# One product per rotation in the S5 scan, 64x64 matmul tiles for its states, and the attention scale moved to ScalarE

## The chip, the cores and the metric

The kernel runs on one core of a Trainium2 chip. The metric is device time in microseconds (us) of one execution, as the median of several; lower is better. Engine names are those of the profile: PE is the matmul engine, PEld its weight loads, DVE the vector engine, ACT the scalar engine, POOL the GpSimd engine, SP the engine that issues most DMAs.

## The reference, cut to what matters

The program computes two decoder layers on 512 tokens of width 1024. Each layer has a mixer (an S5 state-space group of 512 channels beside a differential-attention group of 4 heads) and a SwiGLU channel mixer. The two pieces that the change touches are the S5 recurrence and the last scale of an attention head:

```python
# S5: 32 groups of 16 channels, each with 64 complex states (separate real and imaginary arrays)
bu_re = einsum('blgc,gpc->blgp', u, bb_re); bu_im = einsum('blgc,gpc->blgp', u, bb_im)
# st[t] = lb * st[t-1] + bu[t], complex, for each group and state
y = einsum('blgp,gcp->blgc', st_re, c_re) - einsum('blgp,gcp->blgc', st_im, c_im) + d_skip * u
y = gelu(y);  y = y * sigmoid(y @ glu_w + glu_b)
...
# attention, per head and block of 128 queries
o = (softmax0 - lam * softmax1) @ v
o = o * rsqrt(mean(o * o) + RMS_EPS) * gain
```

## The kernel before

**Scan.** The 512 steps are cut into 64 blocks of 8. Inside a block everything is matmuls with tables (Q brings a block's inputs to the state, M is the block's own response, G brings the state that enters a block to the 8 outputs). Between blocks the state is multiplied by the 8th power of lb. `s5_scan` takes the phase of that factor out: it rotates the block inputs by a table of cosines and sines of k times the phase (k = 0 to 63), runs two real recurrences along k (`tensor_tensor_scan` with the magnitude `dt`), and rotates back. The 32 groups are treated in four quarters q of 8 groups; on the 128 partitions lie two groups of 64 states (g2 = 0, 1), and along the free axis four pairs of groups (a = 0 to 3) by 64 blocks.

A quarter runs in four steps, `inp`, `inT`, `scan` and `sout`. In `scan`, PE writes `vps` (real and imaginary part, 256 columns each) into PSUM. DVE makes four products of 256 columns and two sums for the first rotation, two scans, four products for the way back, and four sums of 64 partitions by 252 columns that write the states S, shifted by one block. S is 1024 columns wide: POOL has cleared it, and the states of g2 = 0 and g2 = 1 stand in different halves, so that `s5_out` can multiply all 128 rows of S by G at once (8 products of 128x128 by 128 columns; each float32 product is two instructions on PE).

**Tables.** `s5_rot` makes the cosines and sines of one quarter (POOL, DVE, ACT) and stores them in DRAM (`sC`, 512 columns). The store is issued from ACT's queue for layer 0 and from POOL's for layer 1. `s5_gen` loads them back into `csl` when a quarter begins. `s5_build` makes Q, G and the kernel of M. Layer 0's tables are built while its own attention starts; layer 1's during the channel mixer of layer 0.

**Buffers.** Tiles with one tag share a few buffers, and a new tile waits until the one whose buffer it takes is done with. `t5` has two buffers of 512 columns; it holds most short-lived tiles of the S5 part (`thl`, `cs`, `btmp`, `ta`, `ksb`, `stmp`, `gl`). `dt` has one of its own. `B` has four of 1024 columns (the inputs `u2`, the outputs `y`, and S), `XS` two of 1024 columns (`UU`, the transposed input, and `wz`, which holds rotated inputs and scanned states).

**Order.** While PE works through the q and k projections, a counter (`tick`) advances, and a table of due times (PLAN) says when the next step of `bld` (tables), `s5`, `att` (attention), `mod` (a column of the modulation: a 512 KB load and a DVE product) and `pf` (a weight unit: load, ACT copy `whi`, DVE difference `wlo`) is issued. An engine runs its instructions strictly in the order in which they are issued to it.

**Attention scale.** In `att_gen`, `scale(h)` computes one factor per query and block (`es`, its power of -1/2 on POOL), multiplies the four blocks of the head's output in PSUM by it on DVE (`on`), and `output(h)` transposes `on` on PE back into the same PSUM bank `po`.

Of the kernel before, what the change touches and what calls it, by code (L numbers as in the profile page):

```python
# [9 lines left out]
F32 = mybir.dt.float32  # L10
# [3 lines left out]
AF = mybir.ActivationFunctionType  # L14
# [48 lines left out]
def trunk_kernel(tc, xT, x, c, pos, modw, modb, wst, s5a, s5bc, s5d, glub, lamv, subw, lng, lnr, out):  # L63
# [3 lines left out]
    with ExitStack() as es:  # L67
# [9 lines left out]
        def u4(tag, shape, dt=F32, name=None):  # L77
            return up.tile(shape, dt, tag=tag, name=name or tag, bufs=BUFS[tag])
# [10 lines left out]
        def sm(shape, name, bufs=2):  # L89
            return sp.tile(shape, F32, tag=name, name=name, bufs=bufs)  # L90
# [80 lines left out]
                                pattern=[[-1, P]], channel_multiplier=1)  # L171
        maskb = cst.tile([P, P], BF16, name="maskb")
        nc.vector.tensor_copy(maskb, maskf)
        onesm = cst.tile([P, P], F32, name="onesm")
        nc.gpsimd.memset(onesm, 1.0)
        mask16 = cst.tile([P, 16], F32, name="mask16")
        nc.vector.tensor_reduce(mask16, ident.rearrange("p (b c) -> p c b", c=16), axis=AX.X, op=ALU.add)
        ebase = cst.tile([P, 16], F32, name="ebase")
# [70 lines left out]
        kd = [dp.tile([4, P, 240], F32, tag="kd", name=f"kd{l}") for l in range(L)]  # L249
        sG = dp.tile([4, P, 1024], F32, tag="sG", name="sG", bufs=1)  # L250
        sQ = dp.tile([4, P, 1024], F32, tag="sQ", name="sQ", bufs=1)
        sC = dp.tile([4, P, 512], F32, tag="sC", name="sC", bufs=1)
        xs = dp.tile([NT, P, D], F32, tag="xs", name="xs", bufs=1)

        def zero_pad(src):
# [244 lines left out]
        def s5_rot(l, q, pm):  # L500

            gs = slice(4 * q, 4 * q + 4)
            sh = [P, 4, 64]
            bg = lambda v: v[:, gs].rearrange("p (g o) -> p g o", o=1).to_broadcast(sh)
            kb = kio.rearrange("p (o k) -> p o k", o=1).to_broadcast(sh)
            thl = t5([P, 2] + sh[1:], name="thl")
            th, tl = thl[:, 0], thl[:, 1]
            tt(th, kb, bg(pm["hi"]), ALU.mult, eng=nc.gpsimd)
            tt(tl, kb, bg(pm["lo"]), ALU.mult, eng=nc.gpsimd)
            cs = t5([P, 2, 4, 64], name="cs")  # L510
            ct, st = cs[:, 0], cs[:, 1]
            flat = lambda v: v.rearrange("p g k -> p (g k)")
            ts(ct, th, INV2PI, ALU.mult, MAGIC, ALU.add)
            ts(ct, ct, MAGIC, ALU.subtract)
            for v, c_ in ((th, -T1), (tl, -T2)):
                stt(flat(v), flat(ct), c_, flat(v), ALU.mult, ALU.add)
            tt(th, th, tl, ALU.add)
            ts(th, th, PI_LO, ALU.min, -PI_LO, ALU.max)
            sincos(ct, st, th, nc.vector)
            getattr(nc, "gpsimd" if l else OPT["CSQ"]).dma_start(sC[q], cs.rearrange("p r g k -> p (r g k)"))  # L520

        tabs = {}

# [44 lines left out]
        def s5_scan(l, q, U, Q, cs):  # L568

            gs = slice(4 * q, 4 * q + 4)  # L570
            ct, st = cs[:, 0], cs[:, 1]
            dt = sm([P, 4, 64], "dt", 1)
            nc.gpsimd.tensor_copy(dt, pms[l]["r8"][:, gs].rearrange("p (g o) -> p g o", o=1).to_broadcast([P, 4, 64]))
            nc.gpsimd.memset(dt[:, :, 0:1], 0.0)
            vps = ps5("vps")
            for ri in range(2):
                for a in range(4):
                    for g2 in range(2):
                        nc.tensor.matmul(vps[64 * g2 : 64 * g2 + 64, ri * 256 + 64 * a : ri * 256 + 64 * a + 64],
                                         Q[:, a, ri, 64 * g2 : 64 * g2 + 64],  # L580
                                         U[:, a, 64 * g2 : 64 * g2 + 64],
                                         start=True, stop=True, tile_position=(0, 64 * g2))
            v = vps.rearrange("p (r a k) -> p r a k", r=2, a=4)
            wz = u4("XS", [P, 4, 4, 64], name="wz")
            tmp = t5([P, 2, 4, 64], name="stmp")
            tt(tmp[:, 0], v[:, 0], ct, ALU.mult)
            tt(tmp[:, 1], v[:, 1], st, ALU.mult)
            tt(wz[:, 0], tmp[:, 0], tmp[:, 1], ALU.add)
            tmp = t5([P, 2, 4, 64], name="stmp")
            tt(tmp[:, 0], v[:, 1], ct, ALU.mult)  # L590
            tt(tmp[:, 1], v[:, 0], st, ALU.mult)
            tt(wz[:, 1], tmp[:, 0], tmp[:, 1], ALU.subtract)
            flat = lambda v_: v_.rearrange("p g k -> p (g k)")
            for ri in range(2):
                nc.vector.tensor_tensor_scan(flat(wz[:, 2 + ri]), flat(dt), flat(wz[:, ri]), 0.0,
                                             op0=ALU.mult, op1=ALU.add)
            S = u4("B", [P, 2, 4, P], name="S")
            nc.gpsimd.memset(S, 0.0)
            for ri in range(2):
                tmp = t5([P, 2, 4, 64], name="stmp")  # L600
                tt(tmp[:, 0], wz[:, 2 + ri], ct, ALU.mult)
                tt(tmp[:, 1], wz[:, 3 - ri], st, ALU.mult)
                for g2 in range(2):
                    rows = slice(64 * g2, 64 * g2 + 64)
                    tt(S[rows, ri, :, 64 * g2 + 1 : 64 * g2 + 64], tmp[rows, 0, :, 0:63], tmp[rows, 1, :, 0:63],
                       ALU.subtract if ri == 0 else ALU.add)
            return S

        def s5_out(q, U, S, G, M, y):
            hh = q % 2  # L610
            ps = ps5("yps")

            for a in range(4):
                for g2 in range(2):
                    nc.tensor.matmul(ps[64 * g2 : 64 * g2 + 64, a * P : (a + 1) * P],
                                     U[:, a, 64 * g2 : 64 * g2 + 64], M[:, 2 * a + g2],
                                     start=a == 0, stop=False, tile_position=(0, 64 * g2))
            for a in range(4):
                for ri in range(2):
                    mm(ps[:, a * P : (a + 1) * P], S[:, ri, a], G[:, a, ri], False, a == 3 and ri == 1)  # L620
            yo = y.rearrange("p i (g c) -> p g i c", g=8)[:, 4 * hh : 4 * hh + 4]

            gl = t5([P, 512], name="gl")
            nc.scalar.activation(gl, ps, AF.Square, scale=GELU_C)
            stt(gl, gl, 1.0, ps, ALU.add, ALU.mult)
            nc.scalar.activation(gl, gl, AF.Tanh, scale=GELU_S)
            stt(gl, gl, 1.0, ps, ALU.add, ALU.mult)
            cp(yo, gl.rearrange("p (a i c) -> p a i c", a=4, i=8), scale=0.5)
# [11 lines left out]
        def s5_gen(l, u2, us, yh, yl):  # L640
            src = u2[0][:, 0:1]
            U, S, Q, C, GM, y = {}, {}, {}, {}, {}, {}

            def inp(q):
                if l:
                    Q[q] = s5_load_q(l, q, us[0][:, 0:1] if q == 0 else src)
                U[q] = s5_in(u2, q)
                C[q] = sm([P, 2, 4, 64], "csl", 1)
                nc.sync.dma_start(C[q].rearrange("p r g k -> p (r g k)"), sC[q])

            def inT(q):
                U[q] = s5_inT(U[q])

            def scan(q):
                if l == 0:
                    Q[q] = tabs[q]["Q"]
                GM[q] = s5_load_gm(l, q, src)
                S[q] = s5_scan(l, q, U[q], Q[q], C[q])

            def sout(q):  # L660
                if q % 2 == 0:
                    y[q // 2] = u4("B", [P, 8, P], name="y")
                s5_out(q, U[q], S[q], *GM[q], y[q // 2])

            def yT(b, ih):
                if (b, ih) == (0, 0):
                    for i in range(2):
                        yh[i] = u4("A1", [P, 2, T], F32R, name="yh")
                        yl[i] = u4("A1", [P, 2, T], F32R, name="yl")
                s5_yT(y[b], b, ih, yh, yl)  # L670

            seq = [(fn, (q,)) for q in range(4) for fn in (inp, inT, scan, sout)]
            seq += [(yT, (b, ih)) for b in range(2) for ih in range(2)]
            for fn, args in seq:
                fn(*args)
                yield
# [42 lines left out]
        def att_gen(qkts, vt, nlam, gain, mix):  # L719
# [57 lines left out]
            def scale(h):  # L777

                g = hd[h]
                ss, q2, po = g["ss"], g["q2"], g["po"]  # L780
                es_ = sm([P, NT], "es", 2)
                tt(es_, ss[:, :, 0], ss[:, :, 0], ALU.mult)
                ts(es_, es_, EPS * P, ALU.mult)
                tt(es_, es_, q2, ALU.add)
                ts(es_, es_, 1.0 / P, ALU.mult)
                tt(es_, es_, mhalf.to_broadcast([P, NT]), ALU.pow, eng=nc.gpsimd)
                on = ta_([P, NT, P], name="on")
                for i in range(NT):
                    ts(on[:, i], po[:, i * P : (i + 1) * P], es_[:, i : i + 1], ALU.mult)
                g["on"] = on  # L790

            def output(h):
# [569 lines left out]
```

## Time and profile before

| | |
|---|---|
| median of 3 runs | 1278.39 us (1275.9 to 1282.51) |
| profiled execution, its own time | 1279.54 us |
| its span in the trace | 1277.8 us |
| busy: PE, DVE, ACT, POOL | 1190.9, 841.6, 478.9, 206.4 us |
| mean granted PE clock | 0.976 of full speed |

The span is what the trace shows from the first instruction to the last; 1.74 us of the execution's own time lie around it. Busy shares are means over stages with different limits, so a stage is read by its own window. In a timeline row stand the start, the time from the first instruction's start to the last one's end, the engine and line, and in brackets the engine's idle time before it with what ended it.

### The profile page before, as it was taken

What the parts mean: (1) busy time and instruction counts of PE and PEld (TensorE: products, weight loads), DVE (VectorE), ACT (ScalarE), POOL (GpSimd) and SP (SyncE); (2) the same over time, 40 slices, a digit from 0 to 9 for tenths busy, and PEclk for the clock granted to TensorE, in tenths of its full rate; (3) what the DMA queues carried; (4) which work ended last, traced back from release to release, by engine and by line L of the source; (5) the groups of instructions that cost most, each with busy time, mean ns of one, the idle gap of its engine ahead of it and who ended that gap; (6) DMA issues with size and microseconds to landing.
All of it is one profiled execution on the core that took longest, in us unless ns stands there. A gap on an engine that the chain in (4) does not pass through costs nothing.

```text
span 1277.8 us, 17430 instructions
## 1 busy us (share of the span) xinstructions
PE 1190.9 (93%) x6608; PEld 992.1 (78%) x6608; DVE 841.6 (66%) x1537; ACT 478.9 (37%) x846; POOL 206.4 (16%) x286
## 2 busy tenths in 40 slices
PE   4768888999999999989899999999999999999997
PEld 3557777688888888867687798878888888888885
DVE  6679999866687576698647557785666222235556
ACT  3413446527322222243346245661733222234330
POOL 8943320001002121132001131100000000000001
PEclk8887999999999999999899999999999999999999
DMA  9654236534665666744333554423463333333241
GB/s 357 226 153 143 65 82 226 158 107 152 195 221 186 226 200 193 252 141 146 117 99 101 186 168 107 131 83 99 151 196 103 98 96 100 99 99 115 66 133 66
DMA packets 66868, 186.57 MB, mean 146 GB/s; under 512 B 7936, under 2 KB 21536, under 8 KB 66784
## 3 DMA queue, kind: packets, MB, share of 16 engines
q1 hardware_dynamic: 62352, 174.88, 43.4%
q0 software_dynamic: 2848, 8.70, 2.1%
q10 hardware_dynamic: 1584, 1.88, 0.5%
q8 instruction: 52, 0.85, 0.3%
q14 instruction: 32, 0.26, 0.1%
HBM read 171.85 MB, written 11.49 MB: 143 GB/s over the span
## 4 chain that ended last, share of the span: by engine, by line
PE 68%; DVE 18%; DMA 4%; POOL 3%; issue 3%; ACT 3%; SPq 0%; DVEq 0%; POOLq 0%; ACTq 0%
PE gps L116 37%; PE dps L116 14%; PE ops L116 4%; PE vps L116 3%; DVE mraw L110 3%; PE ups L116 2%; PE qkps L116 2%; DVE wlo L104 2%; DVE stmp L104 1%; POOL s5tmp L104 1%; DMA mraw<-in_modw 1%; DMA wraw<-in_wst 1%; DVE Gt L104 1%; PE yps L116 1%; PE glups L116 1%
## 5 line engine op out<-in xcount | busy, mean ns | idle before, releaser
L104 DVE TENSOR_TENSOR wlo<-wraw,whi 128x1024 fp32r<-128x1024 f32 x180 | 225.3, 1254 | 266.3 <-ACT whi L113 264.4
L113 ACT ACTIVATE whi<-wraw 128x1024 fp32r<-128x1024 f32 x184 | 194.2, 1058 | 376.6 <-PE gps L116 273.0
L116 PE MATMUL gps<-hT2h,whi 128*128 128x512 f32 (+1 forms) x768 | 286.4, 373 | 0.2
L116 PE MATMUL gps<-hT2l,whi 128*128 128x512 f32 (+1 forms) x768 | 285.7, 372 | 0.0
L116 PE MATMUL gps<-hT2h,wlo 128*128 128x512 f32 (+1 forms) x768 | 285.3, 372 | 0.0
L116 PE MATMUL dps<-whi,ah 128*128 128x512 f32 x704 | 223.7, 397 | 8.2 <-DVE rtmp L104 4.5
L116 PEld LDWEIGHTS gps<-hT2h,whi 128*128 128x128 f32 x768 | 144.6, 188 | 25.8 <-DVE rtmp L104 0.6
L116 PEld LDWEIGHTS dps<-whi,ah 128*128 128x128 f32 x704 | 133.9, 190 | 39.5 <-DVE rtmp L104 6.0
L116 PEld LDWEIGHTS gps<-hT2h,wlo 128*128 128x128 f32 x768 | 144.7, 188 | 25.1
L116 PEld LDWEIGHTS gps<-hT2l,whi 128*128 128x128 f32 x768 | 144.7, 188 | 24.9
L116 PE MATMUL dps<-wlo,ah 128*128 128x512 f32 x352 | 138.5, 393 | 0.0
L110 DVE SCALAR_TENSOR_TENSOR mraw<-mraw,scb 128x1024 f32<-128x1024 f32 x96 | 122.0, 1299 | 1.8 <-DMA mraw<-in_modw 1.6
L113 ACT ACTIVATE ah<-aT 128x512 fp32r<-128x512 f32 x88 | 53.8, 627 | 115.5 <-PE dps L116 93.2
L104 DVE TENSOR_TENSOR ah<-aT,ah 128x512 fp32r<-128x512 f32 x88 | 61.1, 706 | 40.0 <-ACT ah L113 39.6
L116 PEld LDWEIGHTS dps<-wlo,ah 128*128 128x128 f32 x352 | 67.2, 191 | 13.6
L116 PE MATMUL qkps<-whi,hTh 128*128 128x256 f32 x128 | 39.7, 312 | 7.3 <-ACT whi L113 6.5
L116 PE MATMUL ops<-whi,am 128*128 128x512 f32 x128 | 43.4, 398 | 0.0
L116 PE MATMUL qkps<-wlo,hTh 128*128 128x256 f32 x128 | 40.0, 313 | 0.5 <-DVE wlo L104 0.5
L104 POOL TENSOR_TENSOR rs<-rs,mhalf 128x1 f32<-128x1 f32 x16 | 10.8, 676 | 176.8 <-DVE rs L101 176.8
L116 PE MATMUL qkps<-whi,hTl 128*128 128x256 f32 x128 | 39.1, 306 | 0.0
L751 ACT ACTIVATE e<-sps,nm 128x128 f32<-128x128 f32 (+3 forms) x64 | 33.1, 525 | 14.9 <-DVE nm L749 12.8
L116 PE MATMUL qkps<-whi,hTnh 128*128 128x256 f32 x128 | 37.4, 292 | 0.0
(290 smaller groups left out, 1939.4 us busy)
## 6 DMA issues: line engine op xcount, KB each, us to landing
wraw<-in_wst SPq DMA_DIRECT2D x184, 512.0 KB, 3.7
mraw<-in_modw SPq DMA_DIRECT2D x96, 512.0 KB, 4.8
M<-kd SPq DMA_DIRECT2D x64, 64.0 KB, 3.6
gb<-in_lnr SPq DMA_DIRECT2D x8, 512.0 KB, 4.1
xT<-in_xT SPq DMA_DIRECT2D x8, 256.0 KB, 7.1
u<-us SPq DMA_DIRECT2D x32, 64.0 KB, 2.5
csl<-sC SPq DMA_DIRECT2D x8, 256.0 KB, 2.8
x<-in_x SPq DMA_DIRECT2D x4, 512.0 KB, 4.1
```

The lines of the kernel that those rows point to most:

```text
L104: (eng or nc.vector).tensor_tensor(out, a, b, op=op)
L110: nc.vector.scalar_tensor_tensor(out, a, s, b, op0=ALU.mult, op1=ALU.mult, accum_out=acc_out)
L113: nc.scalar.activation(out, in_, AF.Copy, scale=scale)
L116: nc.tensor.matmul(ps, a, b, start=start, stop=stop)
L751: nc.scalar.activation(e[:, m, :n], ps[:, m, :n], AF.Exp, bias=nm[:, m : m + 1], accum_out=ss[:, i, m : m + 1])
```

## The change

- The table of a quarter gets a third part: minus sine, cosine, sine, side by side (768 columns). `s5_rot` makes the minus sine with one more DVE operation into a new `t5` tile and stores it with a second DMA.
- A rotation is one DVE product of 1024 columns: the input (512 columns) is read twice, and the table is read as two overlapping windows of 512 columns. The product `rp` takes a buffer of tag `B`. The first rotation then needs one sum of 512 columns; the second needs two sums of 252 columns over all 128 partitions. The real and imaginary parts are kept in the other order between the two rotations.
- The states S are plain (64 columns per group pair, no zero halves) and overwrite the first half of `wz`. POOL clears only the first column of each block instead of 1024 columns.
- `s5_out` multiplies S by G in tiles of 64 rows by 64 columns of the array, one for each g2: 16 products instead of 8.
- `dt` becomes a `t5` tile; the scan's `stmp` tiles are gone.
- `scale(h)` multiplies the four blocks on ACT instead of DVE.
- An unused constant tile of ones is no longer made.

```diff
-        onesm = cst.tile([P, P], F32, name="onesm")
-        nc.gpsimd.memset(onesm, 1.0)
...
-        sC = dp.tile([4, P, 512], F32, tag="sC", name="sC", bufs=1)
+        sC = dp.tile([4, P, 768], F32, tag="sC", name="sC", bufs=1)
...
-            getattr(nc, "gpsimd" if l else OPT["CSQ"]).dma_start(sC[q], cs.rearrange("p r g k -> p (r g k)"))
+            ns = t5([P, 256], name="ns")
+            ts(ns, flat(st), -1.0, ALU.mult)
+            eng = getattr(nc, "gpsimd" if l else OPT["CSQ"])
+            eng.dma_start(sC[q][:, 256:768], cs.rearrange("p r g k -> p (r g k)"))
+            eng.dma_start(sC[q][:, 0:256], ns)
...
-            dt = sm([P, 4, 64], "dt", 1)
+            dt = t5([P, 4, 64], name="dt")
...
-            wz = u4("XS", [P, 4, 4, 64], name="wz")
-            tmp = t5([P, 2, 4, 64], name="stmp")
-            tt(tmp[:, 0], v[:, 0], ct, ALU.mult)
-            tt(tmp[:, 1], v[:, 1], st, ALU.mult)
-            tt(wz[:, 0], tmp[:, 0], tmp[:, 1], ALU.add)
...
-            S = u4("B", [P, 2, 4, P], name="S")
-            nc.gpsimd.memset(S, 0.0)
-            for ri in range(2):
-                tmp = t5([P, 2, 4, 64], name="stmp")
-                tt(tmp[:, 0], wz[:, 2 + ri], ct, ALU.mult)
-                tt(tmp[:, 1], wz[:, 3 - ri], st, ALU.mult)
-                for g2 in range(2):
-                    rows = slice(64 * g2, 64 * g2 + 64)
-                    tt(S[rows, ri, :, 64 * g2 + 1 : 64 * g2 + 64], tmp[rows, 0, :, 0:63], tmp[rows, 1, :, 0:63],
-                       ALU.subtract if ri == 0 else ALU.add)
+            two = [P, 2, 2, 256]
+
+            def rot_of(v):
+                rows_ = bass.AP(cs.tensor, cs.offset, [cs.ap[0], [256, 2], [256, 2], [1, 256]])
+                pr = u4("B", two, name="rp")
+                tt(pr, v.rearrange("p (o j x) -> p o j x", o=1, j=2).to_broadcast(two), rows_, ALU.mult)
+                return pr
+
+            wz = u4("XS", [P, 4, 256], name="wz")
+            pr = rot_of(vps)
+            tt(wz[:, 0:2], pr[:, :, 0], pr[:, :, 1], ALU.add)
+            d1 = dt.rearrange("p g k -> p (g k)")
+            for o in range(2):
+                nc.vector.tensor_tensor_scan(wz[:, 2 + o], d1, wz[:, o], 0.0, op0=ALU.mult, op1=ALU.add)
+            pr = rot_of(wz[:, 2:4].rearrange("p j x -> p (j x)"))
+            S = wz[:, 0:2].rearrange("p o (g k) -> p o g k", g=4)
+            nc.gpsimd.memset(S[:, :, :, 0:1], 0.0)
+            for o in range(2):
+                po, pj = (pr[:, o, j].rearrange("p (g k) -> p g k", g=4)[:, :, 0:63] for j in range(2))
+                tt(S[:, o, :, 1:64], po, pj, ALU.add)
...
-                    mm(ps[:, a * P : (a + 1) * P], S[:, ri, a], G[:, a, ri], False, a == 3 and ri == 1)
+                    for g2 in range(2):
+                        rows_ = slice(64 * g2, 64 * g2 + 64)
+                        nc.tensor.matmul(ps[rows_, a * P : (a + 1) * P], S[rows_, ri, a], G[rows_, a, ri],
+                                         start=False, stop=a == 3 and ri == 1, tile_position=(64 * g2, 64 * g2))
...
-                C[q] = sm([P, 2, 4, 64], "csl", 1)
-                nc.sync.dma_start(C[q].rearrange("p r g k -> p (r g k)"), sC[q])
+                C[q] = sm([P, 768], "csl", 1)
+                nc.sync.dma_start(C[q], sC[q])
...
-                    ts(on[:, i], po[:, i * P : (i + 1) * P], es_[:, i : i + 1], ALU.mult)
+                    nc.scalar.activation(on[:, i], po[:, i * P : (i + 1) * P], AF.Copy, scale=es_[:, i : i + 1])
```

## Rows read from the trace of the kernel before

**Rows 1.** The page, busy time of each engine and its share.

```profile
PE 1190.9 (93%) x6608; PEld 992.1 (78%) x6608; DVE 841.6 (66%) x1537; ACT 478.9 (37%) x846; POOL 206.4 (16%) x286
```

**Rows 2.** Busy time by stage; first row names columns.

```profile
core 0: us, PE busy (x) PEld busy (x) DVE busy (x) ACT busy (x) POOL busy (x), PEclk, DMA share, GB/s
64.00:110.00 46.00, 34.54 (x234) 30.24 (x232) 35.35 (x77) 10.44 (x20) 18.08 (x23) 0.81 0.50 143
110.00:235.00 125.00, 106.74 (x937) 91.36 (x936) 118.04 (x254) 60.73 (x146) 28.05 (x27) 0.95 0.43 127
235.00:265.00 30.00, 27.82 (x153) 21.11 (x152) 22.03 (x54) 14.14 (x40) 3.49 (x3) 1.00 0.56 173
534.00:612.00 78.00, 70.49 (x364) 56.15 (x362) 68.60 (x109) 29.69 (x46) 23.61 (x25) 0.98 0.47 149
740.00:852.00 112.00, 106.30 (x929) 94.11 (x928) 80.38 (x194) 61.44 (x155) 20.53 (x24) 1.00 0.42 119
```

**Rows 3.** Timeline of DVE: first and last operations of two scans, layer 0.

```profile
110.53 1.08 DVE L104 TENSOR_TENSOR stmp<-vps,csl 128x256 f32<-128x256 f32 x3
...
115.03 1.82 DVE L104 TENSOR_TENSOR S<-stmp 64x252 f32<-64x252 f32 x4
...
141.19 0.76 DVE L104 TENSOR_TENSOR stmp<-vps,csl 128x256 f32<-128x256 f32 x2 [1.42 <-PE vps L579]
...
146.43 2.52 DVE L104 TENSOR_TENSOR S<-stmp 64x252 f32<-64x252 f32 x4
```

**Rows 4.** Groups by form: busy us, mean ns of one, idle before.

```profile
L104 DVE TENSOR_TENSOR wlo<-wraw,whi 128x1024 fp32r<-128x1024 f32 x180 | 225.3, 1254 | 266.3 <-ACT whi L113 264.4 <-DMA M<-kd 1.5
...
L104 DVE TENSOR_TENSOR gluy<-yh,yl 128x512 f32<-128x512 f32 x8 | 5.5, 688 | 0.0
...
L104 DVE TENSOR_TENSOR wz<-stmp 128x256 f32<-128x256 f32 x16 | 6.6, 410 | 0.0
...
L101 DVE TENSOR_SCALAR on<-po,es 128x128 f32<-128x128 f32 x32 | 9.5, 345 | 6.9 <-POOL es L104 6.9
...
L751 ACT ACTIVATE e<-sps,nm 128x128 f32<-128x128 f32 x16 | 5.7, 366 | 5.0 <-DVE nm L749 5.0
...
L598 POOL MEMSET S<- 128x1024 f32 x8 | 7.6, 953 | 0.0
```

**Rows 5.** Instructions of tile wz: duration ns min/median/max.

```profile
L595 DVE TENSOR_TENSOR_SCAN wz<-dt,wz x16: 680/684/2883, 112.2 to 808.1; 128x256 f32<-128x256 f32 x16
```

**Rows 6.** Timeline of PE around a quarter's output, layer 1.

```profile
815.13 1.09 PE L615 MATMUL yps<-M,UU 128*64 128x128 f32 x16
816.15 2.05 PE L116 MATMUL yps<-G,S 128*128 128x128 f32 x16
...
819.38 0.94 PE L747 MATMUL sps<-qk 64*128 64x128 f32 x12
```

**Rows 7.** Timeline of ACT: next quarter's input, then this quarter's output.

```profile
115.15 0.63 ACT L113 ACTIVATE UU<-u 128x512 f32<-128x512 f32 x1 [7.48 <-DVE stmp L104]
...
121.41 0.60 ACT L624 ACTIVATE gl<-yps 128x512 f32<-128x512 f32 x1 [3.56 <-PE yps L116]
```

**Rows 8.** Instructions of tile cs: duration ns min/median/max; landing of its DMA.

```profile
L101 DVE TENSOR_SCALAR cs<-cs x16: 281/294/708, 67.1 to 603.8; 128x256 f32<-128x256 f32 x16
...
L520 POOL DMA_DIRECT2D sC<-cs x4: 562/572/583, 451.9 to 604.6; - x4
...
DMA to landing us min/median/max: 2.0/2.6/4.4
```

**Rows 9.** Timeline of ACT, DVE and POOL where tables are built, layer 0.

```profile
78.09 0.33 ACTq L520 DMA_DIRECT2D sC<-cs  x1
...
78.03 0.22 DVE L104 TENSOR_TENSOR btmp<-s5bc,kre 128x64 f32<-128x64 f32 x1
...
104.54 1.11 POOL L104 TENSOR_TENSOR ta<-pw,s5bc 128x512 f32<-128x512 f32 x1 [4.94 <-DMA sC<-cs]
```

More of the change, by code (lines that the diff above doesn't have):

```diff
@@ L570, in s5_scan @@
             gs = slice(4 * q, 4 * q + 4)
-            ct, st = cs[:, 0], cs[:, 1]
-            dt = sm([P, 4, 64], "dt", 1)
+            dt = t5([P, 4, 64], name="dt")
             nc.gpsimd.tensor_copy(dt, pms[l]["r8"][:, gs].rearrange("p (g o) -> p g o", o=1).to_broadcast([P, 4, 64]))
@@ L582, in s5_scan @@
                                          start=True, stop=True, tile_position=(0, 64 * g2))
-            v = vps.rearrange("p (r a k) -> p r a k", r=2, a=4)
-            wz = u4("XS", [P, 4, 4, 64], name="wz")
-            tmp = t5([P, 2, 4, 64], name="stmp")
-            tt(tmp[:, 0], v[:, 0], ct, ALU.mult)
-            tt(tmp[:, 1], v[:, 1], st, ALU.mult)
-            tt(wz[:, 0], tmp[:, 0], tmp[:, 1], ALU.add)
-            tmp = t5([P, 2, 4, 64], name="stmp")
-            tt(tmp[:, 0], v[:, 1], ct, ALU.mult)
@@ L591, in s5_scan @@
-            tt(tmp[:, 1], v[:, 0], st, ALU.mult)
-            tt(wz[:, 1], tmp[:, 0], tmp[:, 1], ALU.subtract)
-            flat = lambda v_: v_.rearrange("p g k -> p (g k)")
-            for ri in range(2):
-                nc.vector.tensor_tensor_scan(flat(wz[:, 2 + ri]), flat(dt), flat(wz[:, ri]), 0.0,
-                                             op0=ALU.mult, op1=ALU.add)
-            S = u4("B", [P, 2, 4, P], name="S")
-            nc.gpsimd.memset(S, 0.0)
-            for ri in range(2):
-                tmp = t5([P, 2, 4, 64], name="stmp")
-                tt(tmp[:, 0], wz[:, 2 + ri], ct, ALU.mult)
-                tt(tmp[:, 1], wz[:, 3 - ri], st, ALU.mult)
-                for g2 in range(2):
-                    rows = slice(64 * g2, 64 * g2 + 64)
-                    tt(S[rows, ri, :, 64 * g2 + 1 : 64 * g2 + 64], tmp[rows, 0, :, 0:63], tmp[rows, 1, :, 0:63],
-                       ALU.subtract if ri == 0 else ALU.add)
+            two = [P, 2, 2, 256]
```

## The prediction

> **What bounds the kernel now.** I read the page first: PE is busy 93% of the span and DVE 66% [rows 1], which says only that most of the program is PE's. Then the windows by stage, because the edits touch four stages [rows 2]. In 110 to 235 us, layer 0's attention and scans, DVE is busy 118.04 of 125 us (94%) and PE 106.74 at a clock of 0.95: DVE sets the pace there. In 534 to 612 us, where layer 1's last tables are built, DVE is busy 68.60 of 78 (88%) and PE idles 7.5 us. In 740 to 852 us, layer 1's attention and scans, PE is busy 106.30 of 112 and DVE 80.38: PE sets the pace, and no relief of another engine can give more than the 5.7 us in which PE idles. Between 64 and 110 us neither is full (DVE 35.35 of 46, PE 34.54); this stage is a chain of table building. So an edit is worth nearly its DVE time in layer 0's attention, at most a few us in layer 1's, and its waits count in the table building.
>
> **The scan on DVE.** Before, two scans of layer 0 took 115.03 + 1.82 - 110.53 = 6.3 us and 146.43 + 2.52 - 141.19 = 7.8 us of DVE, from first product to last sum [rows 3]; the second includes an operation of the attention. After, seven operations remain, each (but the second scan and the last sum) needing the one before: a product of 1024 columns (1.25 us, from the 1024-column difference), a sum of 512 (0.69), two scans (0.68 each), a product of 1024 (1.25), two sums of 252 (0.41 each, from a 256-column sum) [rows 4, 5]. Together 5.4 us. No row has a DVE operand that is read twice or by overlapping windows, nor 1024 columns of PSUM by SBUF. If that costs nothing, the saving is 6.3 - 5.4 = 0.9 to 7.8 - 5.4 = 2.4 us a quarter; if the product from PSUM took twice its price, 1.25 more, it would be -0.3 to 1.1. I take 1.5: what an operation does is still one element per lane and step, and the four half-partition sums, which stretch to 2.52 us in the second scan, become two. That is 6 us of DVE in each layer. POOL's clearing of S (0.95 us each) goes too [rows 4]; POOL is idle most of that stage, so I count nothing for it.
>
> **The attention scale.** Four DVE operations of 0.345 us, 1.4 us a head, go to ACT, where a 128x128 operation from PSUM with a per-partition operand takes 0.366 us [rows 4]: four take 1.5 us. ACT is busy 60.73 of 125 us in layer 0 and 61.44 of 112 in layer 1 [rows 2], so it has room; but it runs in order, and a 1 us copy ahead of it can delay `on`, then PE's transposes. The chain's length stays the same within 0.1 us, and DVE is relieved of 1.4 us a head: 3 heads inside layer 0's full stage, 4.1 us; 4 heads in layer 1.
>
> **What that relief is worth.** Layer 0: 6 + 4.1 = 10.1 us of DVE. All of it counts if DVE alone sets the pace; but PE has only 18 us of room in 110 to 235, and the last stretch, 235 to 265, has DVE at 22.03 of 30 [rows 2]. I take three quarters: -7.6 us (bounds -10.1 and, by one third, -3.4). Layer 1: 11.5 us of DVE, but PE has 5.7 us to give: I take -2.5 (bounds -5.7 and 0).
>
> **The longer table.** One more DVE operation for each quarter and layer, 0.29 us as the 256-column scalings of `cs` [rows 8], and one more DMA issue: 0.33 us on ACT's queue in layer 0 [rows 9], 0.57 us on POOL in layer 1 [rows 8]. Layer 0 does it in the table building, where ACT's next weight copy is queued behind the issue: 4 x (0.29 + 0.33) = 2.5 us, of which I put 0.5 on the path, since neither engine is full. In layer 1, 4 x 0.29 = 1.2 us of DVE, mostly in or near a stretch that is DVE's own: +1.0. The load of `csl` grows from 256 to 384 KB; it is issued a step ahead of the scan, and I price it at nothing while that step covers it; uncovered, it would cost half of a like transfer's time again, about 1.3 us (half of 2.6) [rows 8].
>
> **The new wait.** The table's third part is a `t5` tile, and `t5` has two buffers. The sequence was thl, cs, next tile: the next tile took thl's buffer, free as soon as ACT had read it. Now it is thl, cs, ns, next tile: ns takes thl's buffer, and the next tile must wait for the store of cs to land. In layer 0 the first products of the table build stand right there: DVE starts `btmp` at 78.03, while ACT issues the store of cs at 78.09 [rows 9]; it lands 2.6 us later (median) [rows 8]. So `btmp` would start at about 78.09 + 2.6 = 80.7, 2.7 us late, and behind it in DVE's queue stand the products of G, on which PE's next tables wait. The third and fourth quarter's tables come right before the next build in the same way; there POOL's `ta` already waits 4.94 us for such a landing [rows 9], so part is paid already: +1.3. Sum +4.0; bounds 0 (other DVE work is issued into the gap: DVE has 10.6 us of idle time in 64 to 110) and +8 (each of three tables costs 2.7). In layer 1, steps of the build lie several us apart and POOL's queue holds the stores; I count the landing as covered. `dt`, now in `t5` too, takes over one of the two buffers until the second scan is done; the `stmp` tiles held both, so I count nothing.
>
> A second wait moves: S now lives in `wz`, so the next quarter's `UU` on ACT can no longer take that buffer when the last product has read it (it did, at 115.15, after 7.48 us of ACT waiting) but only after PE's output product, which ended just before 121.41 [rows 7]. Behind it on ACT are weight copies. This quarter's own `gl` waits for the same PE product, so an order that places `UU` beside `gl` loses nothing; I take 0 (bounds 0 and 6 us once, if the copies stay behind `UU`).
>
> **PE's products.** The old 16 instructions with S took about (2.05 - 0.28)/15 = 0.12 us each, a last 0.28 taken off as the duration of a single one [rows 6]. The new 32 work on two different quarters of the array. Pairs of column tiles, writing the two halves of the same PSUM bank, go at (1.09 - 0.28)/15 = 0.054 us each, and pairs of row tiles, in two different banks, at (0.94 - 0.28)/11 = 0.06 [rows 6]. At that rate 32 take 1.7 to 1.9 us beside 1.8: no change. If the pairs did not overlap, 32 x 0.12 = 3.8 us: +2.0 us a quarter. I take 0, since the two tiles write different partitions.
>
> Here the Trainium skill speaks against the change: TensorEngine Tiling (Array Packing), section Restrictions and Gotchas, says that different row tiles cannot access the same PSUM bank at the same time. The new products are row tiles of one bank; by that rule they would take turns, and the sum would be the one of rival D below. No row of before has such a pair.
>
> **Sum.** -7.6 - 2.5 + 0.5 + 1.0 + 4.0 + 0 = -4.6 us. The profiled execution took 1279.54 us, so its like would take 1274.9; the runs' median is 1.15 us lower, 1278.39, which gives 1273.8. I say 1274.
>
> **Rivals.** About 0.5%, 6.4 us, is what a measurement of this kernel can tell from no change: faster is below 1272.0, slower above 1284.8.
>
> A, the sum above, 1270 to 1279: 0.44.
>
> B, the relief counts whole and the new wait is filled: -10.1 in layer 0, -4 in layer 1, +2.0 for the table: -12, 1266. For it: DVE at 94% for 125 us; against it: a PE near its limit too. 0.22.
>
> C, slower by the two `t5` buffers: the waits for the stores cost 8 + 1.5, and since tables come later, PE idles, falls to the lower of its two clock levels (1.2 instead of 2.4 GHz), and only a third of layer 0's relief (-3.4) arrives, none in layer 1: +6, 1284.5, split evenly around the bound. It decides from the point where the store's landing costs more than DVE saves in layer 0, some 7.6 us. For it: the clock of 0.81 in 64 to 110 and a PE that already lacks work there [rows 2]; against it: DVE's idle time there. 0.22.
>
> D, the 64x64 pairs take turns: +2.0 x 4 = 8 in layer 1, where PE sets the pace, and a quarter of that, 2, in layer 0: -4.6 + 10 = +5.4, 1283.8. For it: no row of a like pair; against it: the pairs of column tiles that share a bank. 0.12.
>
> Faster: B and 0.14 of A, 0.36. Slower: half of C and a little over half of D, 0.11 + 0.07 = 0.18. Same: what is left, 0.46. The range that leaves out no more than 2 in 10 goes from 1264 (B and a little) to 1287 (C and D with their spread).
>
> **What would show it.** Scans of 5.4 us on DVE; `on` on ACT at 0.37 us; the 32 S products in about 2 us and not 4; the first `btmp` of layer 0 waiting for the store of cs; layer 0's attention ending 3 us earlier than 265 us; layer 1's PE idle time in its attention down by 2 to 3 us. The prediction is wrong if the 1024-column product from PSUM costs much over 1.25 us, if no `t5` wait appears, or if ACT's order holds weight copies behind `UU` or `on`.

## The result, and the profile after

The changed kernel takes 1286.24 us (median of 8 executions, 1282.63 to 1290.77), the kernel before 1279.35 us beside it (8 executions). The ratio is 1.0055, 95% interval 1.0038 to 1.0073: 7 us slower. 1274 was forecast, faster; 1286 lies inside the stated range, on the other side.

The page after, the busy time of each engine, to be set against [rows 1]:

```profile
PE 1190.3 (93%) x6736; PEld 990.6 (77%) x6736; DVE 822.4 (64%) x1441; ACT 488.4 (38%) x878; POOL 201.7 (16%) x289
```

DVE lost 19 us of work (841.6 to 822.4), as planned, PE's work is the same, and the kernel is longer. So the question is where 19 us of relief went. The windows over the stretches of [rows 2]:

```profile
64.00:110.00 46.00, 30.88 (x219) 26.45 (x218) 33.05 (x76) 9.42 (x19) 17.93 (x21) 0.81 0.49 154
110.00:235.00 125.00, 106.83 (x1003) 91.33 (x1002) 110.74 (x212) 64.22 (x153) 26.90 (x32) 0.93 0.43 130
235.00:265.00 30.00, 28.23 (x154) 22.04 (x154) 20.99 (x49) 15.54 (x46) 2.47 (x3) 0.94 0.50 159
534.00:612.00 78.00, 73.26 (x373) 58.59 (x371) 68.65 (x111) 29.64 (x46) 25.73 (x29) 0.96 0.46 147
740.00:852.00 112.00, 104.93 (x989) 92.54 (x988) 72.76 (x147) 64.94 (x161) 18.76 (x26) 1.00 0.44 128
```

In 110 to 235 us DVE falls from 118.04 to 110.74 us while PE's busy time stays (106.74, 106.83). Between 64 and 110 us PE does 3.7 us less (34.54, 30.88). In 740 to 852 us DVE is relieved of 7.6 us and PE still does 1.4 us less.

The first scan on DVE's timeline, to be set against [rows 3], and the output products on PE's, against [rows 6]:

```profile
113.03 1.22 DVE L104 TENSOR_TENSOR rp<-vps,csl 128x1024 f32<-128x1024 f32 x1
114.29 0.69 DVE L104 TENSOR_TENSOR wz<-rp 128x512 f32<-128x512 f32 x1
115.08 1.27 DVE L599 TENSOR_TENSOR_SCAN wz<-dt,wz 128x256 f32<-128x256 f32 x2
116.39 1.22 DVE L104 TENSOR_TENSOR rp<-wz,csl 128x1024 f32<-128x1024 f32 x1
117.65 0.75 DVE L104 TENSOR_TENSOR wz<-rp 128x252 f32<-128x252 f32 x2
...
820.55 1.09 PE L614 MATMUL yps<-M,UU 128*64 128x128 f32 x16
821.57 1.96 PE L621 MATMUL yps<-G,wz 64*64 64x128 f32 x32
```

This first scan runs from 113.03 to 118.40, 5.4 us, the sum of the prediction to a tenth; the product of 1024 columns takes 1.22 us whether it reads PSUM or SBUF, and against the 1.25 us of a plain one [rows 4] the operand read twice costs nothing. The other three of layer 0 take 7.1, 6.5 and 6.5 us, with operations of the attention and pauses between theirs; over all four the span is 4.7 us shorter than before, 1.2 a quarter. The 32 products of 64x64 take 1.96 us where the 16 of before took 2.05 [rows 6], and not the 3.8 of taking turns: the pairs overlap in one bank, and rival D is out.

### The profile page after: what moved, and what is told of

The parts are those of the page before. It is cut to its first block, busy times and chain, and to the rows that moved or that the text cites. A ratio compares the mean times of both kernels' runs of the same rounds, so it can differ in the third digit from the quotient of the medians.

```text
span 1285.2 us, 17666 instructions
## 1 busy us (share of the span) xinstructions
PE 1190.3 (93%) x6736; PEld 990.6 (77%) x6736; DVE 822.4 (64%) x1441; ACT 488.4 (38%) x878; POOL 201.7 (16%) x289
## 4 chain that ended last, share of the span: by engine, by line
PE 69%; DVE 17%; DMA 4%; ACT 4%; issue 3%; POOL 1%; SPq 0%; DVEq 0%; ACTq 0%; POOLq 0%
PE gps L116 37%; PE dps L116 14%; PE ops L116 5%; PE qkps L116 3%; DVE mraw L110 3%; PE vps L116 3%; PE ups L116 2%; DVE wlo L104 2%; DMA wraw<-in_wst 1%; DMA mraw<-in_modw 1%; ACT whi L113 1%; DVE ah L104 1%; PE vps L581 1%; PE po L116 1%; DVE rp L104 1%
```

## The waits that took the relief

**Waits for the stores.** Layer 0's table building on POOL, ACT and PE after, against POOL and DVE in [rows 9]; the bracket is the idle time before the instruction and what ended it:

```profile
98.23 1.59 POOL L104 TENSOR_TENSOR thl<-kio,phihi 128x256 f32<-128x256 f32 x1 [7.19 <-DMA sC<-ns]
...
97.04 1.06 ACT L113 ACTIVATE whi<-wraw 128x1024 fp32r<-128x1024 f32 x1 [3.65 <-DMA wraw<-in_wst]
...
98.15 0.80 PE L116 MATMUL qkps<-whi,hTh 128*128 128x256 f32 x2 [8.34 <-ACT whi L113]
```

POOL stands 7.19 us before the fourth quarter's `thl`, whose `t5` buffer comes free only when the store of `ns` has landed. In the kernel before the same instruction stood at 94.43 after 2.48 us, and PE's wait at 96.75 was 6.48 us. PE's 8.34 us is not POOL's wait, though: it ends with the weight copy `whi`, which starts before that `thl` and waits for a weight load that was issued at 88.00 and took 9.0 us to land. How much of POOL's wait reaches PE in layer 0 these rows don't show. At the place that the prediction named, `btmp`, DVE waited only 0.95 us (it starts at 78.51).

Layer 1's table building, on POOL, DVE and PE:

```profile
606.01 0.58 POOL L523 DMA_DIRECT2D sC<-ns  x1 [5.65 <-DVE cs L101]
606.58 0.54 POOL L522 DMA_DIRECT2D sC<-cs  x1
609.28 0.40 POOL L575 COPY dt<-r 128x256 f32<-128x256 f32 x1 [2.16 <-DMA sC<-ns]
609.74 0.10 POOL L576 MEMSET dt<- 128x4 f32 x1
609.82 0.19 POOL L330 COPY G<-ah 128x1 f32<-128x1 f32 x1
...
617.18 0.69 DVE L104 TENSOR_TENSOR rtmp<-dps,G 128x512 f32<-128x512 f32 x1 [5.95 <-DMA G<-gd]
...
617.92 0.79 PE L116 MATMUL dps<-whi,ah 128*128 128x512 f32 x1 [6.92 <-DVE rtmp L104]
```

`dt` here is that of layer 1's first scan, some 135 us ahead of its use. As a `t5` tile it waits 2.16 us for the landing of `ns`, and in POOL's queue behind it stands the copy that releases the load of the gate `G`, which `rtmp` needs, which PE needs: PE waits 6.92 us, and 3.55 at the same place before (612.79). Not all of the difference is POOL's: the load of `G`, issued at 610.03, was used 7.2 us later, and 4.8 us after its issue before (607.29 to 612.04); why it took longer was not followed.

**Waits for the scale.** Layer 1's attention and glu, on POOL, ACT and PE:

```profile
845.73 1.38 POOL L104 TENSOR_TENSOR es<-es,mhalf 128x4 f32<-128x4 f32 x1 [20.03 <-DVE es L101]
...
847.14 1.14 ACT L791 ACTIVATE on<-po,es 128x128 f32<-128x128 f32 x4 [1.53 <-POOL es L104]
848.15 0.61 ACT L113 ACTIVATE qk<-qktp 128x512 f32<-128x512 f32 x1
...
846.41 0.39 PE L116 MATMUL glups<-yh,wlo 128*128 128x512 f32 x1
848.33 0.66 PE L798 MATMUL po<-ident,on 128*128 128x128 f32 x4 [1.53 <-ACT on L791]
```

ACT stands idle 1.53 us until POOL has the power `es`, then scales; PE's next instruction is the transposes of `on`, and it waits 1.53 us too, though 24 products of the glu that need nothing of this come after it in PE's queue. The kernel before waited for `es` as well, but on DVE, and PE had those products first: its transposes at 849.16 waited for nothing.

## The experiments

Theories at the outset: **T**, the waits of the two-buffer `t5` tiles take the relief back; **R1** (later S, Q and Q2), the scale on ACT delays PE; **R2**, the order that the compiler gives all engines moves the times, without any one wait; **R3**, the longer table itself costs. Ratios are to the kernel before on the same chip, with 95% intervals; 0.001 is 1.28 us. The stages in the table are PE's, in the one profiled execution: "layer 0" from the first `qkps` to the first `gps`, "build" from there to layer 1's first `ups`, "layer 1" from there to the last `ops<-whi,yh`.

| kernel | median us | ratio | layer 0 | build | layer 1 |
|---|---|---|---|---|---|
| before | 1279.35 | 1 | 220.3 | 388.0 | 216.7 |
| changed | 1286.24 | 1.0055 | 222.8 | 390.4 | 219.2 |
| e1 `dt` out of `t5` | 1285.47 | 1.0044 (1.0028 to 1.0059) | 223.4 | 389.1 | 219.0 |
| e7 `ns` out | 1279.66 | 1.0003 (0.9991 to 1.0015) | 221.3 | 386.5 | 219.2 |
| e2 both out | 1280.20 | 1.0006 (0.9992 to 1.0020) | 221.6 | 387.7 | 219.3 |
| e3 scale on DVE | 1279.27 | 0.9998 (0.9983 to 1.0014) | 218.6 | 389.2 | 217.4 |
| e5 scale on DVE in layer 1 | 1283.15 | 1.0032 (1.0018 to 1.0045) | 221.1 | 390.2 | 216.8 |
| e6 both out, scale on DVE | 1274.51 | 0.9964 (0.9949 to 0.9978) | 214.9 | 387.6 | 216.7 |
| e9 e6, layer 0's scale on ACT | 1277.61 | 0.9996 (0.9984 to 1.0008) | 218.9 | 387.2 | 216.8 |
| e12 e6, `ns` in `ta` | 1274.51 | 0.9966 (0.9951 to 0.9980) | 215.6 | 387.7 | 216.7 |
| e15 e12, `dt` in `t5` | 1276.32 | 0.9975 (0.9963 to 0.9988) | 213.3 | 386.8 | 216.8 |
| e4 before, scale on ACT | 1281.96 | 1.0017 (1.0002 to 1.0031) | 217.7 | 386.8 | 219.9 |
| e10 before, 64x64 | 1278.07 | 0.9993 (0.9979 to 1.0007) | 219.0 | 385.5 | 218.6 |
| e11 before, `dt` in `tm` | 1279.64 | 1.0009 (0.9995 to 1.0022) | 218.1 | 385.3 | 216.5 |
| e8 minus sine at the load | 1279.22 | 0.9998 (0.9985 to 1.0011) | 219.9 | 386.8 | 216.6 |
| e14 half the scale on ACT | 1278.44 | 0.9997 (0.9989 to 1.0006) | 221.2 | 388.4 | 217.0 |
| e17 e12, scale on ACT | 1282.45 | 1.0034 (1.0021 to 1.0046) | 219.3 | 389.4 | 219.2 |
| e13 e17, later transposes | 1284.33 | 1.0041 (1.0027 to 1.0055) | 223.2 | 389.4 | 219.1 |
| e16 e13, `on` behind `qk` | 1281.49 | 1.0031 (1.0018 to 1.0045) | 221.9 | 387.4 | 217.5 |

Single executions scatter by some 3 us. The four profiles of the old scan differ by 2.6 us in layer 0 and by 2.7 in the build, so differences of that size in these two columns show nothing alone; the medians decide there. Layer 1's column is steady to about half a us, but for e10.

**e1, e7, e2: the tiles out of `t5`.** One line each; `t2` makes a tile of the three `tm` buffers.

```
-            dt = t5([P, 4, 64], name="dt")
+            dt = t2([P, 4, 64], name="dt")
-            ns = t5([P, 256], name="ns")
+            ns = t2([P, 256], name="ns")
```

> The decays dt back out of the two t5 buffers (into the three tm buffers, which are idle at that time). Theory T (waits of the two-buffer t5 tiles eat the relief of DVE): layer 1's first dt no longer stands on POOL behind the landing of the store of ns, the gate's load starts as early as before, and the first rtmp comes 3 us earlier or more, so about 1283.2, 3 below the changed kernel. Rival R1 (the scale on ACT delays PE): no change, 1286.2. Rival R2 (the order that the compiler gives all engines, with no one wait behind it): no change or any sign, since most of the order stays.

> Only the table's third part ns out of t5; dt stays there, the scale stays on ACT. Theory T: layer 0's wait goes (2 to 3 us), dt's wait in layer 1 is no longer for the landing of ns but for a tile that is free: 1281 to 1283. If the kernel with both out (1280.2) owes its time to the two together or to its order: 1284 to 1286.

> Both dt and the table's third part ns out of t5 (into tm). Theory T: the 3 us in layer 1's table building and in layer 0 up to the 2.1 us by which its attention ends late both go: 1281 to 1283, and with the relief of DVE left at 1 to 2 us no more than level with the kernel before. Rival R1: 1286 as the changed kernel. Rival R3 (the longer table itself, its operation, its DMA and its load, costs the time): 1286 too, since all of that stays.

`ns` alone is worth 1.0055 - 1.0003, 6.6 us, more than T had; `dt` alone 0.8 to 1.4 us, less than the 3 of T, and the intervals do not part it from nothing; both together no more than `ns`. POOL and PE in e7, and PE in e1, where `ns` is still in `t5`:

```profile
92.96 0.69 POOL L104 TENSOR_TENSOR thl<-kio,phihi 128x256 f32<-128x256 f32 x1 [2.48 <-ACT cs L227]
...
602.67 0.47 POOL L575 COPY dt<-r 128x256 f32<-128x256 f32 x1 [4.52 <-ACT cs L227]
...
605.61 0.72 POOL L330 COPY G<-ah 128x1 f32<-128x1 f32 x1 [0.57 <-ACT ah L113]
...
95.37 0.79 PE L116 MATMUL qkps<-whi,hTh 128*128 128x256 f32 x2 [5.50 <-ACT whi L113]
...
612.61 0.79 PE L116 MATMUL dps<-whi,ah 128*128 128x512 f32 x1 [3.91 <-DVE rtmp L104]
```

```profile
96.49 0.80 PE L116 MATMUL qkps<-whi,hTh 128*128 128x256 f32 x2 [5.60 <-ACT whi L113]
...
617.44 0.79 PE L116 MATMUL dps<-whi,ah 128*128 128x512 f32 x1 [4.04 <-DVE rtmp L104]
```

POOL's wait of 5.1 to 7.2 us for `ns` in layer 0 is in all four profiles with `ns` in `t5` (changed, e1, e3, e5) and gone in e7. PE's wait for `whi` falls from 8.34 to 5.50, but that is no sign of it: in e1, e3 and e5 it is 5.60 to 5.94 with `ns` still in `t5`. In the build PE waits 6.92, 5.32 and 7.18 us in the three profiles with both tiles in `t5` (changed, e3, e5), 4.04 without `dt` (e1) and 3.91 without `ns` (e7), where `dt`, still in `t5`, waits for nothing that lands. So that the place of `ns` costs several us is shown by the medians: 6.6 us with `dt` in `t5`, 4.9 without it (e1 to e2). Of this 3 us is a wait that PE can be seen to lose, in the build; where the rest lies, and whether it is the wait at all and not the order that comes with the other tag (R2), is not shown. e1 has lost nearly as much of that PE wait and gained at most 1.4 us, so a wait of PE isn't worth its whole length either.

**e3, e4, e5: the scale.**

```
-                    nc.scalar.activation(on[:, i], po[:, i * P : (i + 1) * P], AF.Copy, scale=es_[:, i : i + 1])
+                    ts(on[:, i], po[:, i * P : (i + 1) * P], es_[:, i : i + 1], ALU.mult)
```

in both layers (e3), with `if l:` ahead of it in layer 1 only (e5), and the other way round in the kernel before (e4).

> Only the scale of the attention output goes back to DVE. Theory T: the table's waits stay, DVE does 1.4 us more for each head, of which little counted: 1285 to 1289. Rival R1 (PE waits for on behind ACT's exponentials and copies, 2.2 us seen at 838 to 856 us and 1.8 us at 245 us): 1282 to 1284, with those two waits gone.

> The kernel before with only the scale moved to ACT. Theory T: between level and 2.5 us faster (1277 to 1279.4 beside 1279.4). Rival R1: 2 to 4 us slower (1281.5 to 1283.5), with PE waiting for on behind ACT in both layers.

> The changed kernel with the scale on DVE in layer 1 only; layer 0 keeps it on ACT. Theory S (in layer 1 the scale on ACT costs 2.5 us of its own, by the waits of PE for yl and on, and the rest of the loss lies in layer 0 and in layer 1's table building): 1283.5, 2.5 below the changed kernel, with layers 0 and the build late as before. Rival R2 (the times of layer 0 go with the order that the compiler gives and not with the edits): any time between 1280 and 1287, with layer 0 moved though none of its code is.

R1 wins here, with more than it had. The scale on ACT costs 7.3 us in the changed kernel (1.0055 to 0.9998), 2.9 in layer 1 (e5) and 4.3 in layer 0 (e5 to e3). With the old scan it costs 2.2 us, by the table all in layer 1 (219.9 against 216.7). In layer 0 PE waits for `on` there with the scale on either engine: 0.57 us at 219.91 and 1.88 at 247.07 in the kernel before, 2.18 and 0.72 in e4.

**e6, e9: the scan alone, and layer 0's scale.** e6 is e2 with e3's edit; e9 puts it back on ACT with `if l == 0`.

> The new scan and the 64x64 products alone: dt and ns out of t5, the scale on DVE. If the losses add up by stage (layer 0 1 to 3 us, layer 1's building 1.5 us, layer 1's glu stretch 2.5 us), nothing is left of them but the relief of DVE: 1276 to 1278, 1.5 to 3.5 below the kernel before. If the relief of DVE is worth nothing because PE has its backlog of q and k products anyway: 1279 to 1281, level.

> The fastest version so far (dt and ns out of t5, scale on DVE) with layer 0's scale on ACT again. If the scale on ACT costs PE's time in layer 0 too, without the waits for the table: 2 to 3 us more than that version, about 1277 (ratio 0.998 to 0.9985). If it costs only in layer 1: 1274.5 (0.9965), or a little less, as DVE is relieved of 4 us there.

Without the waits and the scale the change is 4.6 us faster than the kernel before (0.9964). Layer 0's scale on ACT costs 4.1 us of it, more than expected, with no wait for a store in play.

**e12, e15, e8: other ways to the same scan.** e12 has `ns` from `ta_` and `dt` from `t2`; e15 leaves `dt` in `t5`. e8 stores 512 columns and has POOL make the third part:

```
-                nc.sync.dma_start(C[q], sC[q])
+                nc.sync.dma_start(C[q][:, 256:768], sC[q])
+                ts(C[q][:, 0:256], C[q][:, 512:768], -1.0, ALU.mult, eng=nc.gpsimd)
```

> The fastest version so far with ns in the ta buffers and not in tm, where the loads of s5bc and dt wait for its landing on POOL (2.3 and 4.5 us seen at 96.1 and 102.8 us). If these waits count: 1 to 2 us less, 1272.5 to 1273.5. If they are covered: level with that version, 1274.5.

> The fastest version with dt back in t5 and only ns (in ta) out of it, scale on DVE. Theory T as it stands now (dt costs only because it waits behind the landing of ns): level with the fastest version, 0.9955 to 0.9975. If dt in t5 costs on its own: 0.5 to 1 us more, 0.9975 to 0.998.

> As the run with dt out of t5 and the scale on DVE, but no third part is computed, stored and loaded: POOL makes the minus sine from the loaded table. If the longer table still cost something (one DVE operation and one DMA issue for each quarter, 0.5 to 1.5 us in all): 1275 to 1277; if not, the time of the run that stores it.

`ns` may live in either tag (e12 as e6), so the waits that e12 was to remove were covered; `dt` in `t5` costs 1.2 us by the medians, on the border of the two expectations, and the intervals of e12 and e15 overlap. e8 missed: 4.7 us above e6, by the table in layer 0 (219.9 against 214.9). Why POOL's way costs that was not followed, so e8 puts no price on the longer table. As the cause of the loss R3 is out by e2 and e6, which keep that table.

**e10, e11: the 64x64 products alone, and a neutral edit.**

```
-                    mm(ps[:, a * P : (a + 1) * P], S[:, ri, a], G[:, a, ri], False, a == 3 and ri == 1)
+                    for g2 in range(2):
+                        rows_ = slice(64 * g2, 64 * g2 + 64)
+                        nc.tensor.matmul(ps[rows_, a * P : (a + 1) * P], S[rows_, ri, a, rows_], G[rows_, a, ri],
+                                         start=False, stop=a == 3 and ri == 1, tile_position=(64 * g2, 64 * g2))
```

e11 is `dt = t2(...)` in the kernel before, in place of a buffer of its own.

> The kernel before with the products of S as 32 tiles of 64x64 and nothing else. Rival D (the pairs in one PSUM bank take turns): 4 us more or above, yps groups of 3.8 us instead of 2. If they overlap, as the trace of the changed kernel has it (32 in 1.92 us): level with before, within 1.5 us.

> The kernel before with dt in the tm buffers and not in a buffer of its own: by every price here worth nothing. Rival R2 (the order given by the compiler moves layer 0 by some us whatever is edited): 2 us or more off level, on either side. Otherwise level within 1.3 us.

Both are level: rival D is out a second time, and R2 in its wide form too, since edits without a price moved the median by about 1 us. The 1.9 us by which e10's one profile is longer in layer 1 stay unexplained.

**e14, e17, e13, e16: why the scale on ACT costs.** ACT starts `on` the moment `es` is there, so its speed is not it. Two theories were left: PE's compiled order puts the transposes too early (O), or ACT's queue, held by `on`, holds up what stands behind it (Q). e17 is e12 with the scale on ACT. e13 holds the transposes behind the PE instructions written before them, which moves layer 1's third head only; e16 orders the same head's `on` behind the next head's `qk` copies. e14 has `if i >= 2` ahead of the ACT form.

```
+                with queued({pe: marks()[pe]}):
                     for i in range(NT):
                         nc.tensor.transpose(po[:, i * P : (i + 1) * P], g["on"][:, i], ident)
...
+                        tc.add_manual_dep(ins, qkc[h + 1], NOSYNC, reason="order")
```

> The fastest version (dt in tm, ns in ta) with two of the four scalings of each head on DVE and the last two on ACT. PE's compiled order then puts the transposes as late as with all four on DVE (95, 43, 20, 12, 48, 46, 51, 15 products behind the head's last product with v). Theory O: level with the fastest version, ratio 0.9955 to 0.9975, with the relief of DVE nearly free. Theory Q: half of the price of the scale on ACT, ratio 0.9985.

> dt in tm and ns in ta with the scale on ACT and nothing else: the base of the two runs with later transposes. If ns in ta is as good as in tm (as it is with the scale on DVE): ratio 1.0006 as the run with both in tm, and the later transposes did harm. If ns in ta costs with the scale on ACT, where on and wT stand in the same two buffers: 1.003 to 1.005, and the later transposes did nothing.

> dt and ns out of t5, the scale on ACT in both layers, and the four transposes of on held in PE's order behind every PE instruction that the program writes before them. In the compiled order this moves one head only: layer 1's third, whose transposes now come 51 products after the head's last product with v and not 18. Theory O (what costs is PE's order, which puts the transposes ahead of their data, and not ACT): PE's wait of 1.5 us for on in layer 1's glu stretch goes, and about that much of the time of the run with both out of t5 and the scale on ACT (1280.2, ratio 1.0006): ratio 0.999. Theory Q (on is late because ACT's queue or ACT's operation is slow): no change, 1.0006.

> As the run with the later transposes (scale on ACT, dt in tm, ns in ta), with the four on operations also ordered on ACT behind the next head's two qk copies; in the compiled order this moves layer 1's third head alone. Theory Q2 (ACT works its queue in order, stands 1.5 us before on until POOL's power of es is there, and what PE needs next, here the second qk copy, stands behind it): with neither the transposes nor the qk copy held up, layer 1's stage from ups to the last ops goes from 219.1 to 217.5 us or less, the level of the kernels with the scale on DVE (216.5 to 217.4). Theory O (the early transposes alone): no change from the run before, 219.1.

ACT and PE in e13, layer 1's third head:

```profile
846.05 1.14 ACT L791 ACTIVATE on<-po,es 128x128 f32<-128x128 f32 x4 [1.52 <-POOL es L104]
847.07 0.61 ACT L113 ACTIVATE qk<-qktp 128x512 f32<-128x512 f32 x1
...
847.73 0.49 PE L749 MATMUL sps<-qk 64*128 64x128 f32 x4 [1.54 <-ACT qk L113]
...
854.56 0.66 PE L800 MATMUL po<-ident,on 128*128 128x128 f32 x4
```

The transposes no longer wait, but PE waits the same 1.54 us at the next head's products, for the `qk` copy that stands behind `on` in ACT's queue. ACT and PE in e16:

```profile
842.25 0.60 ACT L113 ACTIVATE qk<-qktp 128x512 f32<-128x512 f32 x1 [0.76 <-PE qktp L732]
843.31 1.15 ACT L792 ACTIVATE on<-po,es 128x128 f32<-128x128 f32 x4
...
843.07 0.49 PE L750 MATMUL sps<-qk 64*128 64x128 f32 x4
849.92 0.66 PE L804 MATMUL po<-ident,on 128*128 128x128 f32 x4
```

Both waits are gone and layer 1's stage is 217.5, as Q expected, 1.6 less than e13's and nearly that of the scale on DVE. So in layer 1's third head it is both together, the order of two in-order queues, as far as one profile of each kernel shows it: the medians of e17, e13 and e16 lie within 1.3 us and their intervals overlap. The first head's wait for `on` is still there in e16 (1.16 us at 791.88). For layer 0 this is not shown: there PE waits for `on` 1.13 us at 182.28 and 1.75 at 245.24 in the changed kernel, nothing over half a us in e6; that is 2.9 of the 4.1 to 4.3 us. e14, which has one of those waits left (1.63 us at 245.61), costs 0.0031 of the 0.0068 between e12 and e17: nearly half, as Q had it, though its 0.9997 is above the 0.9985 that Q gave, and not the nothing of O. e17 and e13 are 3.6 and 4.5 us above e2, from which they differ in the tag of `ns` and, in e13, the later transposes; with the scale on DVE the tag made no difference. Why it does with the scale on ACT is open. e13 and e17 are not parted, so no harm of e13's edit is shown.

## Why the prediction was wrong

The step that failed first is **the attention scale**: "it has room; but it runs in order ... The chain's length stays the same within 0.1 us, and DVE is relieved". The duration was right (0.367 us against 0.366), ACT's room was there, and the chain is as long as before. But the wait for POOL's power moved with the operation from DVE's queue to ACT's, and on ACT copies that PE needs next stand behind it. That is shown in layer 1; in layer 0 the price is measured and its cause open. The step was given as a relief, 4.1 us of the 10.1 in layer 0 and nearly half of layer 1's; it cost 4 us in layer 0 and 1.3 to 2.9 in layer 1. The prediction saw the place ("a 1 us copy ahead of it can delay `on`"; a sign of being wrong if "ACT's order holds weight copies behind `UU` or `on`") and put it at nothing without a reason; what stood behind `on` was the `qk` copy.

**The new wait** was right in kind, and its +4.0 is near the 4.3 us that both tiles are worth with the scale on DVE (e3 to e6) and short of the 6.6 of e7; but its places were in part the wrong ones: it was put on layer 0's `btmp` and the later tables, and "In layer 1 ... I count the landing as covered". Seen as a wait of PE it is 3.0 us in layer 1's build (6.92 to 3.91), where `dt` ("I count nothing") joined the two. In layer 0 `btmp` waited 0.95 us and not 2.7; the long wait was POOL's 7.19 us at the fourth quarter's `thl`, and what of it reaches PE stays open. With `ns` in `ta` and the scale on ACT it was only 1.3 (e1 to e17), which the intervals do not part from nothing.

**What that relief is worth** held in layer 0 for the scan's share. Three quarters of 6 us is 4.5; e6, e12 and e15 have 214.9, 215.6 and 213.3 us there, mean 214.6, against 219.1 for the three profiles of the old scan with the scale on DVE: 4.5. That it fits to a tenth is luck, with scans that saved 4.7 us and not 6 and a column that scatters by 2.6. The medians, 3.2 to 4.6 us by these three kernels, bear the size out. In layer 1 the relief gave nothing (216.7 and 216.7) where 2.5 was forecast: its lower bound.

**The scan** (1.2 us saved a quarter, 1.5 forecast) and **the products** (+0) were right within a us or two of the whole; **the longer table** was priced by no run. The 0.28 us that the products' sum takes off is not in [rows 6]. The `UU` copy came at 118.63 and not at 115.15 [rows 7], after PE's products of `M` with the old `UU` (1.83 us of waiting) and not, as forecast, after those of S; no wait of PE showed behind it. The load of `csl` landed in a median of 3.1 us, and in 2.8 before.

Of the rivals, C named one of the two mechanisms and nearly the right time, 1284.5; the nearness is luck, since its sum has nothing for the scale, which makes about half of the loss. On rival D's rule, the Trainium skill's TensorEngine Tiling (Array Packing), Restrictions and Gotchas: the trace does not agree for 64x64 tiles on two different quarters of the array, 32 in 1.96 us in one bank, and the measurement decides.

The loss splits so: e6 is -4.6; the scale on ACT adds 5.4 (e2), the tiles in `t5` a further 6.3 (e2 to the changed kernel), together 7.1. These are steps of one path and must add up. By the other path the tiles come first with 4.3 (e3) and the scale adds 7.3, so the two cost some 2 us more together than apart, which the intervals do not part from nothing. That e6 meets the -4.6 of the forecast is luck too: the sum there had +4.0 for the waits and some -4 for the scale's relief, and e6 has neither.

## What to carry to other kernels

An operation moved to an engine with room takes its wait along: ask what ends last before it, and what stands behind it in the queue of the engine it goes to. A tile that a DMA reads should not share a two-buffer tag with tiles of the steps right after it (3 to 7 us here), and a tile made far ahead of its use can, in such a tag, hold up the releases of loads behind it in its engine's queue (PE's 6.92 us in the build; in the median at most 1.4). The version to keep is the new scan with `ns` and `dt` in `tm` and the scale on DVE: 1274.5 us, faster than both (0.9964).

## What the runs showed of the hardware

The kernels with the new scan ran layer 0 at a slightly lower granted clock: a mean of 0.92 over 78 to 300 us in their fifteen profiles (0.89 to 0.94), 0.94 in the four of the old scan (0.93 to 0.95). The difference lies in two stretches: 0.82 in 132 to 156 us and 0.79 in 156 to 176, against 0.93 and 0.93; in 110 to 132 us it is the other way, 0.93 against 0.90. The windows of the kernel before, of the changed one, of e15 and of e16, 132 to 156 and 156 to 176 us (the third number from the end is the clock):

```profile
132.00:156.00 24.00, 18.32 (x185) 15.78 (x183) 22.43 (x42) 7.74 (x25) 5.34 (x6) 0.93 0.37 85
156.00:176.00 20.00, 16.08 (x178) 14.16 (x176) 17.87 (x46) 9.92 (x22) 7.07 (x7) 0.91 0.26 75
```

```profile
132.00:156.00 24.00, 19.41 (x207) 16.70 (x207) 21.10 (x34) 9.24 (x26) 7.82 (x9) 0.86 0.41 107
156.00:176.00 20.00, 13.50 (x172) 11.59 (x172) 18.49 (x39) 9.50 (x24) 7.89 (x9) 0.91 0.25 84
```

```profile
132.00:156.00 24.00, 18.84 (x207) 16.01 (x207) 21.36 (x37) 9.25 (x23) 7.13 (x9) 0.93 0.40 108
156.00:176.00 20.00, 15.44 (x179) 13.62 (x180) 18.44 (x40) 9.14 (x23) 6.04 (x9) 0.83 0.33 96
```

```profile
132.00:156.00 24.00, 19.85 (x187) 16.14 (x187) 19.75 (x34) 7.14 (x18) 6.94 (x9) 0.72 0.39 108
156.00:176.00 20.00, 14.27 (x163) 12.38 (x164) 18.52 (x36) 7.91 (x20) 6.87 (x7) 0.74 0.30 92
```

A stretch at 0.72 stood more than half of the time, 0.28 of 0.50, at the lower of the two levels, 1.2 GHz. What PE did before it fell is wait for the third and the fourth table (in e16 3.93 us before 135.09 and 4.72 before 163.55; before, 3.87 and 2.68): in e16 PE is idle from 132 to 134 us, where the granted clock has a mean of 0.91, and from 134 to 146 us it is 0.50. Of the changed kernel's executions the longest, 1290.77 us, has the lowest mean clock, 0.969, and the shortest, 1282.63 us, the highest, 0.976. So part of what DVE saves in layer 0 may come back as a slower PE; how much of a median it makes was not separated.
